# Pacing the sums' transfers by landed weight blocks, and ending the last row tile in two column halves

## The chip, the cores and the metric

The kernel runs on one core of one Trainium2 chip. The metric is the device time of one execution in microseconds (us).

## What is computed

One layer of a hybrid decoder trunk for 512 positions and 1024 channels, all in float32. Only the last part matters for the change:

```python
def conv_ffn(h, w_up, conv_w, w_down):
    up = causal_dwconv(h @ w_up, conv_w)
    gate, val = jnp.split(up, [D_FF], axis=-1)
    return (jax.nn.silu(gate) * val) @ w_down
...
    mix = jax.nn.sigmoid(ga) * y_a + jax.nn.sigmoid(gb) * y_b
    x = x + mix @ w_o[l]
    h = rmsnorm(x, norm_ffn_g[l])
    x = x + conv_ffn(h, w_up[l], ffn_conv_w[l], w_down[l])
    return rmsnorm(x, norm_final_g)
```

Ahead of it stand the projections of the normed input (`w_in`), a gated delta rule, and the products with `w_a_out` and `w_b_out`.

## The kernel before

Each product is made of three matmuls of rounded parts (high by high, high by low, low by high), so every weight block is split on the chip: ScalarE casts it to a high part `wh` (line 140), VectorE subtracts that to get the low part `wl` (line 141). The work is a list of jobs. A job has one weight block of 1 MB, loaded by SyncE's queue (SP) into one of two `raw` buffers, and a `use` that issues its matmuls. `run_jobs` goes through the list: while job i computes, block i+1 is split and block i+2 is loaded. Every 2048 columns of matmul a `tick` takes one step from several queues of small tasks.

Many products save multiplications by Strassen-like forms. Some jobs (`sum_job`) form the sums of weight quarters on VectorE from `raw` (line 161), and put several accumulations into the left half L and the right half R of one PSUM bank A. Between two of them VectorE reads the right half of A (line 283), and the matmuls that follow write the left half:

```python
            def s12():
                act.copy(out=u[:, L], in_=A[:, L])
                dve.tensor_tensor(out=u[:, R], in0=A[:, R], in1=u[:, L], op=ALU.add)
...
            while not done.done:
                advance(evacs, 1)
            times(A[:, L], "12", quarter(1, 0), False)
```

For `w_o` and `w_down` the sums of quarters are formed in DRAM instead, by 112 transfers of 256 KB that GpSimd (POOL) issues (line 1036; `ov`, `ol` for `w_o`, `dv`, `df`, `dl` for `w_down`), most of them adding to what is there. `Sums.form` yields twice after each, and `tick` steps that queue, `adds`, once. On POOL itself nothing ties a transfer to a tick: each waits only for one of eight landing semaphores (DMASW0 to 7) to be free, and for sums that it reads.

The program's order is: delta rule and its projections (to about 300 us), then 24 jobs of `w_in`, `w_a_out` and `w_b_out` (about 310 to 530 us), the product with `w_o` (to 610 us), 22 jobs of `w_up` (to 820 us), and `w_down` in jobs of a 512-column form.

The end is the last `w_down` job, `use_l`: for row tiles 2 and 3 it adds 12 matmuls of 512 columns to the bank of the left half (columns 0 to 511) of that tile; the right half was finished earlier (`fin2_hi`). Then `fin2` runs for each tile: VectorE adds the bank to `x1` (line 1536), ScalarE squares it in place and sums (line 1537), VectorE multiplies by the final gain (1538) and folds the sum into `r` (1541), POOL takes r to the power -1/2 (1543), VectorE scales one half and ScalarE the other (1544, 1545), and SP stores both (1547).

Of the kernel before, what the change touches and what calls it, by code (L numbers as in the profile page):

```python
# [9 lines left out]
F32 = mybir.dt.float32  # L10
# [19 lines left out]
Y_F = (5, 4, 6, 3)  # L30
WARM = 3
WQ = 12
Y_M = 10


# [24 lines left out]
def layer_kernel(ctx, tc, x, norm_mix_g, w_in, w_ab, conv_a_w, gdn_conv_w, gdn_A_log, gdn_dt_bias,  # L60
# [64 lines left out]
    class Block:  # L125
        def __init__(self, src, quarter=(4, P)):
            self.src, self.quarter = src, quarter
            self.raw, self.ready, self.lead = None, False, 2
            self.wh, self.wl = {}, {}

        def load(self):
# [52 lines left out]
    class FormBlock(Block):  # L184
        def __init__(self, runs, names, lead, place):
            super().__init__(None, (S,))
            self.runs, self.names, self.lead, self.place = runs, names, lead, place

        def load(self):
            if self.raw is not None:  # L190
# [13 lines left out]
    def run_jobs(jobs):  # L204
        jobs[1][0].load()
        for i, (block, use) in enumerate(jobs):
            Task(block.split()).finish()
            drain(splits)
            if i + 1 < len(jobs):
                splits.append(Task(jobs[i + 1][0].split()))  # L210
            for j, (later, _) in enumerate(jobs[i + 2:i + 5]):
                if later.lead >= j + 2:
                    later.load()
            use(block.wh, block.wl)


    def piece(w, j, k):
# [797 lines left out]
    class Sums:  # L1015
# [205 lines left out]
        put(xs, slot, 2, 2, 1, xv[:, :, 0, 0])  # L1221
        yield

    def times(o, xs, slot, i, tau, wh, wl, start=False, stop=False, free=False):
        xh, xl = (e[:, slot, i, tau * P:(tau + 1) * P] for e in xs)
        for k, (a, b) in enumerate(((xl, wh), (xh, wl), (xh, wh))):
            mm(o, a, b, start and k == 0, stop and k == 2, free)
# [6 lines left out]
    def times_b(banks, xs, slot, names, tau, wh, wl, q=None, start=False, stop=False):  # L1234
        for name, i in names:
            o, w = banks["11" if name == "21" else name][tau], name if q is None else (name, q)
            times(o, xs, slot, i, tau, wh[w], wl[w], start and name != "21", stop, name == "21")

    def open_banks(banks, names):
        for name in names:  # L1240
# [189 lines left out]
    for g in range(NF // 2):  # L1430
        def up_job(i, c, plain, pre=None):
            if plain:
                return col_job(w_up, i, lambda: st["h2"], c, pre)
            return sum_job(w_up, i, lambda: st["h2"], hsums, c, pair_out)

        last = g == NF // 2 - 1
        gj = up_job(g, gate_c(g), g < 2 or last, (lambda: splits.append(prep_d(prep_a, 0))) if last else None)
        vj = up_job(NF // 2 + g, val_c(g), True)
        jobs += [(gj[0], first_gate), (vj[0], first_val)] if g == 0 else [gj, vj]


# [43 lines left out]
    def use_b(p):  # L1485
        def use(wh, wl):
            if p % 2 == 0 and p // 2 + 1 < N7 // 2:
                splits.append(prep_d(prep_b, p // 2 + 1))
            for name in (*FORMS_T, *FORMS_B):
                for tau in range(2):  # L1490
                    times_b(d_banks, xs(), p % 4, (name,), tau, wh, wl)
            if p == N7 - LAST - 1:
                splits.append(prep_d(prep_b, N7 // 2 - 1))
        return use


    def use_t(q):
# [5 lines left out]
                    fin2(tau, [d_banks["11"][tau], d_banks["22"][tau]])  # L1503
        return use

    def use_l(wh, wl):
        for tau in range(2):
            for i in range(LAST):
                times_b(d_banks, xs(), (N7 - LAST + i) % 4, FORMS_B, tau, wh, wl, i, False, i == LAST - 1)
            fin2(tau + 2, [d_banks["v4"][tau]])  # L1510

    def fin2_hi(t):
        cvp, x1, a = st["cvp"], st["x1"], d_banks["r"][t - 2]
# [10 lines left out]
        yield  # L1524

    def fin2(t, acc):
        cvp, x1 = st["cvp"], st["x1"]
        ss = cvp.tile([P, 2], F32, tag="ss", name=nm("ss"))
        if t < 2:
            o = pair_out()  # L1530
            y, r = [o[:, sl] for sl in HALVES], cvp.tile([P, 1], F32, tag="r", name=nm("r"))
        else:
            y, r = st["y", t], st["r", t]
        for hf, a in enumerate(acc):
            sl = HALVES[hf]
            dve.tensor_tensor(out=x1[:, t, sl], in0=x1[:, t, sl], in1=a, op=ALU.add)  # L1536
            act.activation(out=a, in_=x1[:, t, sl], func=AF.Square, accum_out=ss[:, hf:hf + 1])  # L1537
            dve.tensor_tensor(out=y[hf], in0=x1[:, t, sl], in1=st["gfn"][:, sl], op=ALU.mult)
            if hf < len(acc) - 1:
                dve.tensor_scalar(r, ss[:, hf:hf + 1], 1.0 / D, EPS, op0=ALU.mult, op1=ALU.add)  # L1540
        dve.scalar_tensor_tensor(out=r, in0=ss[:, len(acc) - 1:len(acc)], scalar=1.0 / D, in1=r,  # L1541
                                 op0=ALU.mult, op1=ALU.add)
        pool.tensor_tensor(out=r, in0=r, in1=nhalf[:, 0:1], op=ALU.pow)  # L1543
        dve.tensor_scalar(y[0], y[0], r, None, op0=ALU.mult)
        act.activation(out=y[1], in_=y[1], func=AF.Copy, scale=r)  # L1545
        for sl, e in zip(HALVES, y):
            nc.sync.dma_start(out=out2[t * P:(t + 1) * P, sl], in_=e)


    def down_place(i):  # L1550
# [69 lines left out]
```

## Time and profile before

| | us |
|---|---|
| median of 3 runs (970.35 to 973.03) | 971.42 |
| the profiled execution | 968.61 |
| its span, first to last instruction | 966.9 |
| TensorE (PE) busy | 954.4 |
| VectorE (DVE) busy | 743.9 |
| ScalarE (ACT) busy | 506.3 |
| GpSimd (POOL) busy | 137.1 |

The profiled execution is 1.7 us longer than its span and 2.8 us shorter than the median. A busy PE need not be at its peak, since matmuls overlap; the pace of matmuls is read from their starts.

### The profile page before, as it was taken

The numbers are of one execution on the slowest core, as the hardware profiler recorded it, in microseconds if no ns is written. First come the engines' busy times: TensorE is split into PE (matmuls) and PEld (weight loads), VectorE is DVE, ScalarE is ACT, GpSimd is POOL, SyncE is SP. The second block draws the span as 40 slices with busy tenths as digits, with TensorE's granted clock in tenths as the row PEclk, the third lists the DMA queues.
The fourth block names the chain that finished last, engine by engine and source line by source line (L and its number), as shares of the span: only waits on it lengthen the run. The fifth ranks groups of instructions, "written<-read, shape, count | busy, mean of one in ns | idle before, by whom it ended". The sixth has DMA issues, their size and how long they took to land. (4 is left out here: it accounts for less than half of the span.)

```text
span 966.9 us, 16043 instructions
## 1 busy us (share of the span) xinstructions
PE 954.4 (99%) x6166; PEld 826.9 (86%) x6166; DVE 743.9 (77%) x1397; ACT 506.3 (52%) x1071; POOL 137.1 (14%) x213
## 2 busy tenths in 40 slices
PE   8999999999999999999999999999999999999996
PEld 6888887987878889899988888998889999888885
DVE  6868686896635968799773479999988888969785
ACT  7795556575444434344651235645645455546463
POOL 3330300202002334234320000100000000000000
PEclk9999999999999999999999999999999999999999
DMA  6443312222222989999995235432232323177342
GB/s 226 156 138 115 100 53 88 74 75 75 55 86 76 226 228 252 252 200 260 275 260 150 87 107 220 164 119 88 88 131 87 129 90 132 44 253 235 99 132 87
DMA packets 51628, 138.10 MB, mean 143 GB/s; under 512 B 21691, under 2 KB 22112, under 8 KB 42848
## 3 DMA queue, kind: packets, MB, share of 16 engines
q1 hardware_dynamic: 39008, 107.72, 32.5%
q0 software_dynamic: 12544, 29.37, 14.8%
q8 instruction: 48, 0.79, 0.3%
q14 instruction: 28, 0.23, 0.1%
HBM read 133.64 MB, written 32.78 MB: 172 GB/s over the span
## 5 line engine op out<-in xcount | busy, mean ns | idle before, releaser
L108 PE MATMUL ps<-hT,wh 128*128 128x512 f32 (+1 forms) x1104 | 318.6, 368 | 1.2 <-DVE u L283 0.8
L140 ACT CAST wh<-raw 128x512 fp32r<-128x512 f32 x350 | 203.6, 618 | 214.3 <-PE ps L108 141.0
L141 DVE TENSOR_TENSOR wl<-raw,wh 128x512 fp32r<-128x512 f32 x350 | 232.3, 688 | 62.4 <-ACT wh L140 60.2
L108 PEld LDWEIGHTS ps<-hT,wh 128*128 128x128 f32 x1104 | 196.9, 189 | 30.1 <-DVE u L283 1.0
L108 PE MATMUL ps<-hT,wl 128*128 128x512 f32 (+1 forms) x552 | 195.2, 362 | 0.0
L108 PE MATMUL ps<-h,wh 128*128 128x512 f32 (+1 forms) x704 | 177.9, 341 | 0.3 <-DVE h L1317 0.3
L108 PEld LDWEIGHTS ps<-h,wh 128*128 128x128 f32 x704 | 122.4, 189 | 15.5 <-DVE h L1317 0.5
L108 PEld LDWEIGHTS ps<-hT,wl 128*128 128x128 f32 x552 | 104.4, 189 | 13.8
L108 PE MATMUL ps<-h,wl 128*128 128x512 f32 (+1 forms) x352 | 114.7, 341 | 0.0
L108 PE MATMUL ps<-wh,xs 128*128 128x512 f32 x312 | 96.2, 389 | 0.0
L108 PEld LDWEIGHTS ps<-h,wl 128*128 128x128 f32 x352 | 66.7, 190 | 7.6
L108 PEld LDWEIGHTS ps<-wh,xs 128*128 128x128 f32 x312 | 58.6, 188 | 12.1
L108 PE MATMUL ps<-wl,xs 128*128 128x512 f32 x156 | 60.7, 389 | 0.0
L108 PE MATMUL ps<-ts,wh 128*128 128x256 f32 x320 | 59.2, 283 | 0.0
L328 DVE SCALAR_TENSOR_TENSOR cv<-ps,wA,cv 128x511 f32<-128x511 f32 (+2 forms) x72 | 53.2, 741 | 4.0 <-ACT cv L325 3.8
L140 ACT CAST wh<-raws 128x512 fp32r<-128x512 f32 x66 | 39.2, 619 | 26.2 <-PE ps L108 12.1
L141 DVE TENSOR_TENSOR wl<-raws,wh 128x512 fp32r<-128x512 f32 x66 | 42.8, 685 | 12.1 <-ACT wh L140 12.1
L108 PEld LDWEIGHTS ps<-ts,wh 128*128 128x128 f32 x320 | 50.6, 192 | 0.0
L1543 POOL TENSOR_TENSOR r<-r,nhalf 128x1 f32<-128x1 f32 x4 | 2.2, 540 | 338.2 <-PE ps L108 331.2
L161 DVE TENSOR_TENSOR raw<-raw 128x512 f32<-128x512 f32 x72 | 49.4, 686 | 0.9
L108 PE MATMUL ps<-us,wh 128*128 128x256 f32 x256 | 47.4, 283 | 0.0
L1036 POOL DMA_DIRECT2D dv<-in_w_down_dram x50 | 35.4, 712 | 58.9 <-issue 58.4
(309 smaller groups left out, 1549.8 us busy)
## 6 DMA issues: line engine op xcount, KB each, us to landing
raw<-in_w_in_dram SPq DMA_DIRECT2D x35, 1024.0 KB, 5.5
raw<-in_w_up_dram SPq DMA_DIRECT2D x22, 1024.0 KB, 4.9
dv<-in_w_down_dram POOLq DMA_DIRECT2D x50, 256.0 KB, 7.8
raws<-dv SPq DMA_DIRECT2D x8, 768.0 KB, 7.0
ov<-in_w_o_dram POOLq DMA_DIRECT2D x20, 256.0 KB, 7.1
raws<-in_w_down_dram SPq DMA_DIRECT2D x10, 512.0 KB, 5.1
raw<-in_w_a_out_dram SPq DMA_DIRECT2D x4, 1024.0 KB, 7.7
raw<-in_w_b_out_dram SPq DMA_DIRECT2D x4, 1024.0 KB, 8.5
```

The source lines that it names most:

```text
L108: pe.matmul(o, lhsT=a, rhs=b, start=start, stop=stop, skip_group_check=free)
L140: act.copy(out=wh, in_=src)
L141: dve.tensor_tensor(out=wl, in0=src, in1=wh.bitcast(F32), op=ALU.subtract)
L161: dve.tensor_tensor(out=r[q], in0=a, in1=b, op=op)
L328: dve.scalar_tensor_tensor(out=dst[:, sh:], in0=src[:, :S - sh], scalar=wcol(j), in1=dst[:, sh:], op0=ALU.mult, op1=ALU.add)
L1036: tc.keep_in_program_order(pool.dma_start(out=self.at(g, to), in_=src, **kw))
L1543: pool.tensor_tensor(out=r, in0=r, in1=nhalf[:, 0:1], op=ALU.pow)
```

## The change

Transfers: `adds` is no longer stepped by `tick`. Ahead of the `use` of job i, `feed` makes POOL copy one element of the block of job i+2 (it has to have landed for that) and then issue the next three transfers. It does so where that block is a plain one (`fed`: all of `w_in`, `w_a_out`, `w_b_out`, and `w_up` from its second pair on). There are 38 such copies.

Tail: `use_l` writes its own ending. Tile 3 gets its left half in two halves of 256 columns, 12 matmuls each, and `fin2`'s steps for that tile are made once per half; VectorE, ScalarE, POOL and SP keep the order in which the code is written. The last store goes out on ScalarE's queue. `fin2` is left for tiles 0 and 1 with the same instructions. The `stop` flag set at an earlier job issues nothing.

```diff
@@ tick
         advance(sums_of, 1)
-        advance(adds, 1)
@@ run_jobs
                 if later.lead >= j + 2:
                     later.load()
+            if adds and i + 2 < len(jobs) and jobs[i + 2][0].fed:
+                feed(jobs[i + 2][0].raw)
             use(block.wh, block.wl)
+    def feed(raw):
+        el = raw[0:1, 1].rearrange("p k n -> p (k n)") if len(raw.shape) == 4 else raw[0:1, 1]
+        tc.keep_in_program_order(pool.tensor_copy(out=gate, in_=el[:, 0:1]))
+        advance(adds, FEED)
@@ Sums.form
                         tc.keep_in_program_order(pool.dma_start(out=self.at(g, to), in_=src, **kw))
                         yield
-                        yield
@@ use_l
-        for tau in range(2):
-            for i in range(LAST):
-                times_b(d_banks, xs(), (N7 - LAST + i) % 4, FORMS_B, tau, wh, wl, i, False, i == LAST - 1)
-            fin2(tau + 2, [d_banks["v4"][tau]])
+        def part(t, e, cols, between):
+            a, r = d_banks["v4"][t - 2], st["r", t]
+            ss = st["cvp"].tile([P, 2], F32, tag="ss", name=nm("ss"))
+            for i in range(LAST):
+                times_b(d_banks, xs(), (N7 - LAST + i) % 4, FORMS_B, t - 2, wh, wl, i, False, i == LAST - 1, cols)
+            dve.tensor_tensor(out=x1[:, t, cols], in0=x1[:, t, cols], in1=a[:, cols], op=ALU.add)
+            act.activation(out=a[:, cols], in_=x1[:, t, cols], func=AF.Square, accum_out=ss[:, e:e + 1])
+            between()
+            dve.scalar_tensor_tensor(out=r, in0=ss[:, e:e + 1], scalar=1.0 / D, in1=r, op0=ALU.mult, op1=ALU.add)
+        def between():
+            mult(3, slice(0, HS))
+            scale(2, 1, False, nc.sync)
+            scale(2, 0, True, nc.sync)
+        with tc.manual_schedule(engines={mybir.EngineType.DVE, mybir.EngineType.Activation, mybir.EngineType.Pool,
+                                         mybir.EngineType.SP}):
+            part(2, 0, slice(0, S), lambda: mult(2, slice(0, S)))
+            power(2)
+            part(3, 0, slice(0, HS), between)
+            part(3, 1, slice(HS, S), lambda: None)
+            power(3)
+            mult(3, slice(HS, S))
+            scale(3, 0, False, nc.sync)
+            scale(3, 1, True, nc.scalar)
```

On POOL, around the end of `w_o`'s sums and the start of `w_down`'s, before (a name in brackets behind "waits" is the semaphore waited for):

```order
L1036 DMA ol<-in_w_o_dram 128x512 [waits DMASW0_49]
L1036 DMA ol<-in_w_o_dram 128x512 [waits DMASW1_49]
L1036 DMA ol<-in_w_o_dram 128x512 [waits DMASW2_49]
L1036 DMA ol<-in_w_o_dram 128x512 [waits DMASW3_49]
L1036 DMA dv_371<-in_w_down_dram 128x512 x2
L1036 DMA dv_372<-in_w_down_dram 128x512 x2
L1036 DMA dv_373<-in_w_down_dram 128x512 [waits DMASW4_49]
```

and of the change (DMAHW is the landing of a block on SP's queue):

```order
L223 COPY gate<-raw_5142 1x1 [waits DMAHW4_49,Pool_49]
L1046 DMA ol<-in_w_o_dram 128x512 [waits DMASW2_49]
L1046 DMA ol<-in_w_o_dram 128x512 [waits DMASW3_49]
L1046 DMA dv_372<-in_w_down_dram 128x512
L223 COPY gate<-raw_5286 1x1 [waits DMAHW5_49,Pool_49]
L1046 DMA dv_372<-in_w_down_dram 128x512
L1046 DMA dv_373<-in_w_down_dram 128x512 x2
L223 COPY gate<-raw_5422 1x1 [waits DMAHW6_49,Pool_49]
```

A copy that waits for a weight block now stands ahead of each three transfers; their own order is the same. 21 copies with 63 transfers come ahead of the `w_o` stage's powers on POOL, and 17 copies with the other 49 transfers behind them, among the jobs of `w_up`.

On PE, at the end of the program, the change puts 24 matmuls of 256 columns into the bank `ps_9764` of tile 3, where 12 of 512 columns without any wait stood. These are the end of the first half and the start of the second:

```order
L108 MATMUL ps_9764<-wh_10149,xs_9112 128x256
L108 MATMUL ps_9764<-wl_10150,xs_9111 128x256
L108 MATMUL ps_9764<-wh_10149,xs_9111 128x256
L108 MATMUL ps_9764<-wh_10109,xs_9112 128x256 [waits Activation_49]
L108 MATMUL ps_9764<-wl_10110,xs_9111 128x256
L108 MATMUL ps_9764<-wh_10109,xs_9111 128x256
```

The first matmul of the second half waits for ScalarE; its operands `wh_10109` and `xs_9112` were used 12 matmuls earlier without a wait.

On VectorE, the end of the program before (tile 2 from the third row on, tile 3 from `ps_9725` on):

```order
L1536 TENSOR_TENSOR x_6441<-x_6441,ps_9724 128x512 [waits PE_49]
L1544 TENSOR_SCALAR o_10123<-o_10123,r_10124 128x512 [waits Pool_49]
L1538 TENSOR_TENSOR y_9803<-x_6441,gfn 128x512 [waits DVE_49]
L1541 SCALAR_TENSOR_TENSOR r_9805<-ss_10150,r_9805 128x1 [waits Activation_49]
L1544 TENSOR_SCALAR y_9803<-y_9803,r_9805 128x512 [waits Pool_49]
L1536 TENSOR_TENSOR x_6441<-x_6441,ps_9725 128x512 [waits PE_49]
L1538 TENSOR_TENSOR y_9827<-x_6441,gfn 128x512 [waits DVE_49]
L1541 SCALAR_TENSOR_TENSOR r_9829<-ss_10172,r_9829 128x1 [waits Activation_49]
L1544 TENSOR_SCALAR y_9827<-y_9827,r_9829 128x512 [waits Pool_49]
```

and of the change:

```order
L1544 SCALAR_TENSOR_TENSOR r_9844<-ss_10179,r_9844 128x1 [waits Activation_49]
L1541 TENSOR_TENSOR x_6414<-x_6414,ps_9764 128x256 [waits PE_49]
L1523 TENSOR_TENSOR y_9866<-x_6414,gfn 128x256 [waits DVE_49]
L1530 TENSOR_SCALAR y_9843<-y_9843,r_9844 128x512 [waits Pool_49]
L1544 SCALAR_TENSOR_TENSOR r_9868<-ss_10197,r_9868 128x1 [waits Activation_49]
L1541 TENSOR_TENSOR x_6414<-x_6414,ps_9764 128x256 [waits PE_49]
L1544 SCALAR_TENSOR_TENSOR r_9868<-ss_10218,r_9868 128x1 [waits Activation_49]
L1523 TENSOR_TENSOR y_9866<-x_6414,gfn 128x256 [waits DVE_49]
L1530 TENSOR_SCALAR y_9866<-y_9866,r_9868 128x512 [waits DVE_49,Pool_49]
```

Tile 3's first addition has moved ahead of tile 2's scaling, and there are now two additions and two folds into `r` for tile 3. Before these rows the two programs have the same rows on PE, VectorE, ScalarE and SP.

## Rows read from the trace of the kernel before

**Rows 1.** The page: PE's share, and DMA engines' busy tenths in 40 slices.

```profile
PE 954.4 (99%) x6166; PEld 826.9 (86%) x6166; DVE 743.9 (77%) x1397; ACT 506.3 (52%) x1071; POOL 137.1 (14%) x213
...
DMA  6443312222222989999995235432232323177342
```

**Rows 2.** Windows of 20 us: stretch, length, busy by engine (count), clock, DMA.

```profile
380.00:400.00 20.00, 19.25 (x148) 18.50 (x147) 15.08 (x27) 7.95 (x17) 7.82 (x13) 1.00 0.99 285
420.00:440.00 20.00, 20.00 (x169) 20.00 (x168) 17.96 (x32) 8.27 (x18) 7.60 (x11) 1.00 0.95 202
700.00:720.00 20.00, 20.00 (x129) 18.30 (x128) 17.71 (x30) 10.30 (x20) 0.00 (x0) 1.00 0.30 106
```

**Rows 3.** Timeline of ACT, DVE and PE, 390 to 396 us (start, length).

```profile
390.77 1.14 ACT L140 CAST wh<-raw 128x512 fp32r<-128x512 f32 x2 [4.47 <-DMA raw<-in_w_in_dram]
...
392.75 2.15 DVE L161 TENSOR_TENSOR raw<-raw 128x512 f32<-128x512 f32 x3
...
393.89 0.64 PE L108 MATMUL ps<-hT,wh 128*128 128x256 f32 x4
394.81 0.42 DVE L283 TENSOR_TENSOR u<-ps,u 128x256 f32<-128x256 f32 x1
...
395.28 0.39 PE L108 MATMUL ps<-hT,wh 128*128 128x256 f32 x1 [0.76 <-DVE u L283]
```

**Rows 4.** DMA issues (median us to landing): 340 to 520, 381 to 382, 660 to 820 us; queue of 340 to 520.

```profile
q0 software_dynamic: 10622, 24.79, 66.7%
...
dv<-in_w_down_dram POOLq DMA_DIRECT2D x50, 256.0 KB, 7.8
raw<-in_w_in_dram SPq DMA_DIRECT2D x11, 1024.0 KB, 8.4
...
raw<-in_w_in_dram SPq DMA_DIRECT2D x1, 1024.0 KB, 9.2
...
raw<-in_w_up_dram SPq DMA_DIRECT2D x16, 1024.0 KB, 4.9
```

**Rows 5.** Timeline of the last 9 us (start, length).

```profile
958.93 0.39 PE L108 MATMUL ps<-wh,xs 128*128 128x512 f32 x1
959.10 0.16 DVE L1541 SCALAR_TENSOR_TENSOR r<-ss,r 128x1 f32<-128x1 f32 x1 [0.28 <-ACT ps L1537]
959.91 0.49 DVE L1544 TENSOR_SCALAR y<-y,r 128x512 f32<-128x512 f32 x1 [0.65 <-POOL r L1543]
960.32 0.68 DVE L1536 TENSOR_TENSOR x<-x,ps 128x512 f32<-128x512 f32 x1
...
961.09 0.60 ACT L1537 ACTIVATE ps<-x 128x512 f32<-128x512 f32 x1 [0.46 <-DVE x L1536]
961.63 0.19 ACT L1537 ACTIVATION_READ_ACCUMULATOR ps<-x 128x1 f32 x1
961.85 0.16 DVE L1541 SCALAR_TENSOR_TENSOR r<-ss,r 128x1 f32<-128x1 f32 x1
962.09 0.54 POOL L1543 TENSOR_TENSOR r<-r,nhalf 128x1 f32<-128x1 f32 x1 [2.21 <-DVE r L1541]
962.66 0.72 ACT L1545 ACTIVATE y<-y,r 128x512 f32<-128x512 f32 x1 [0.85 <-POOL r L1543]
...
963.18 0.81 SPq L1547 DMA_DIRECT2D out_dram<-y  x2
```

**Rows 6.** Half-width operations on a bank, 300 to 520 us (ns min/median/max).

```profile
L282 ACT COPY u<-ps x10: 360/372/374, 359.2 to 472.7; 128x256 f32<-128x256 f32 x10
L283 DVE TENSOR_TENSOR u<-ps,u x10: 416/417/425, 359.8 to 473.1; 128x256 f32<-128x256 f32 x10
```

**Rows 7.** Windows at the end, columns as in the second group.

```profile
962.00:963.00 1.00, 0.00 (x0) 0.00 (x0) 0.34 (x2) 0.34 (x1) 0.54 (x1) 0.59 0.67 250
...
964.50:965.00 0.50, 0.00 (x0) 0.00 (x0) 0.00 (x0) 0.00 (x0) 0.00 (x0) 0.50 1.04 389
965.00:965.50 0.50, 0.00 (x0) 0.00 (x0) 0.00 (x0) 0.00 (x0) 0.00 (x0) 0.50 0.81 303
```

More of the change, by code (lines that the diff above doesn't have):

```diff
@@ L32 @@
 WQ = 12
+FEED = 3
 Y_M = 10
@@ L186, in __init__ @@
             super().__init__(None, (S,))
-            self.runs, self.names, self.lead, self.place = runs, names, lead, place
+            self.runs, self.names, self.lead, self.place, self.fed = runs, names, lead, place, False
         def load(self):
@@ L1222, in prep_b, with times @@
         yield
-    def times(o, xs, slot, i, tau, wh, wl, start=False, stop=False, free=False):
+    def times(o, xs, slot, i, tau, wh, wl, start=False, stop=False, free=False, cols=slice(0, S)):
         xh, xl = (e[:, slot, i, tau * P:(tau + 1) * P] for e in xs)
         for k, (a, b) in enumerate(((xl, wh), (xh, wl), (xh, wh))):
-            mm(o, a, b, start and k == 0, stop and k == 2, free)
+            mm(o[:, cols], a, b[:, cols], start and k == 0, stop and k == 2, free)
     def times_a(banks, xs, slot, wh, wl, start, stop):
@@ L1232, in times_a, with times_b @@
                 times(banks[name][tau], xs, slot, i, tau, wh[name], wl[name], start, stop)
-    def times_b(banks, xs, slot, names, tau, wh, wl, q=None, start=False, stop=False):
+    def times_b(banks, xs, slot, names, tau, wh, wl, q=None, start=False, stop=False, cols=None):
         for name, i in names:
             o, w = banks["11" if name == "21" else name][tau], name if q is None else (name, q)
-            times(o, xs, slot, i, tau, wh[w], wl[w], start and name != "21", stop, name == "21")
+            times(o, xs, slot, i, tau, wh[w], wl[w], start and name != "21", stop, name == "21" or bool(cols),
+                  cols or slice(0, S))
     def open_banks(banks, names):
@@ L1438, in layer_kernel @@
         vj = up_job(NF // 2 + g, val_c(g), True)
+        gj[0].fed = vj[0].fed = g > 0
         jobs += [(gj[0], first_gate), (vj[0], first_val)] if g == 0 else [gj, vj]
@@ L1490, in use @@
                 for tau in range(2):
-                    times_b(d_banks, xs(), p % 4, (name,), tau, wh, wl)
+                    times_b(d_banks, xs(), p % 4, (name,), tau, wh, wl, None, False,
+                            p == N7 - LAST - 1 and name in FORMS_B)
             if p == N7 - LAST - 1:
@@ L1506, in use_l, with mult, scale, power @@
     def use_l(wh, wl):
-        for tau in range(2):
-            for i in range(LAST):
-                times_b(d_banks, xs(), (N7 - LAST + i) % 4, FORMS_B, tau, wh, wl, i, False, i == LAST - 1)
-            fin2(tau + 2, [d_banks["v4"][tau]])
+        x1, gfn = st["x1"], st["gfn"]
+        def mult(t, cols):
+            dve.tensor_tensor(out=st["y", t][0][:, cols], in0=x1[:, t, cols], in1=gfn[:, cols], op=ALU.mult)
+        def scale(t, hf, on_act, queue):
+            y, r = st["y", t][hf], st["r", t]
+            if on_act:
+                act.activation(out=y, in_=y, func=AF.Copy, scale=r)
+            else:
+                dve.tensor_scalar(y, y, r, None, op0=ALU.mult)
+            queue.dma_start(out=out2[t * P:(t + 1) * P, HALVES[hf]], in_=y)
+        def power(t):
+            pool.tensor_tensor(out=st["r", t], in0=st["r", t], in1=nhalf[:, 0:1], op=ALU.pow)
+        def part(t, e, cols, between):
+            a, r = d_banks["v4"][t - 2], st["r", t]
+            ss = st["cvp"].tile([P, 2], F32, tag="ss", name=nm("ss"))
+            for i in range(LAST):
+                times_b(d_banks, xs(), (N7 - LAST + i) % 4, FORMS_B, t - 2, wh, wl, i, False, i == LAST - 1, cols)
[17 more added lines that the diff above has]
+            scale(3, 1, True, nc.scalar)
     def fin2_hi(t):
@@ L1526, in fin2 @@
     def fin2(t, acc):
-        cvp, x1 = st["cvp"], st["x1"]
+        cvp, x1, y = st["cvp"], st["x1"], pair_out()
         ss = cvp.tile([P, 2], F32, tag="ss", name=nm("ss"))
[L1529 to L1542, printed above, removed]
+        r = cvp.tile([P, 1], F32, tag="r", name=nm("r"))
+        for hf, sl in enumerate(HALVES):
+            dve.tensor_tensor(out=x1[:, t, sl], in0=x1[:, t, sl], in1=acc[hf], op=ALU.add)
+            act.activation(out=acc[hf], in_=x1[:, t, sl], func=AF.Square, accum_out=ss[:, hf:hf + 1])
+            dve.tensor_tensor(out=y[:, sl], in0=x1[:, t, sl], in1=st["gfn"][:, sl], op=ALU.mult)
+            if hf == 0:
+                dve.tensor_scalar(r, ss[:, 0:1], 1.0 / D, EPS, op0=ALU.mult, op1=ALU.add)
+        dve.scalar_tensor_tensor(out=r, in0=ss[:, 1:2], scalar=1.0 / D, in1=r, op0=ALU.mult, op1=ALU.add)
         pool.tensor_tensor(out=r, in0=r, in1=nhalf[:, 0:1], op=ALU.pow)
[L1544 to L1547, printed above, removed]
+        dve.tensor_scalar(y[:, HALVES[0]], y[:, HALVES[0]], r, None, op0=ALU.mult)
+        act.activation(out=y[:, HALVES[1]], in_=y[:, HALVES[1]], func=AF.Copy, scale=r)
+        for sl in HALVES:
+            nc.sync.dma_start(out=out2[t * P:(t + 1) * P, sl], in_=y[:, sl])
     def down_place(i):
```

3 lines of the change are left out of this document (2 added, 1 removed).

## The prediction, made before the changed kernel was run

> **What bounds the kernel now.** I read the page first. TensorE is busy for 954.4 of 966.9 us, so only what PE loses between its first and last matmul, and what lies outside them, can be won [rows 1]. The DMA line of the same page is near full in slices 14 to 21 (of 24.2 us each), some 190 us in which the 112 transfers of the sums are under way beside the weight blocks. The second view is the windows. At 420 to 440 us, inside that stretch, PE has no idle time and starts 169 matmuls of 256 columns, one per 0.118 us; that is its pace when nothing holds it. At 380 to 400 us it is idle for 0.75 us with the DMA engines at 0.99. At 700 to 720 us, among the jobs of `w_up`, the DMA share is 0.30 and PE is full [rows 2]. So the crowded stretch costs PE one short stall.
>
> The third view, the timeline, shows that stall. ScalarE waits 4.47 us for a block of `w_in` and starts its split at 390.77. VectorE then has the block's sums to make until 394.9, and its read of bank A (L283) comes only at 394.81, behind them. The four matmuls from 393.89 start 0.12 apart, so the next was due at 394.37; it starts at 395.28 and lasts 0.39 instead of 0.28 [rows 3]. Price: 0.91 + 0.11 = 1.0 us. That block took 9.2 us from issue to landing; 11 blocks of `w_in` in the stretch took 8.4 in the median, 16 of `w_up` later 4.9 [rows 4]. The block is late because it shares the DMA engines with the sums.
>
> The fourth view is the end. The last matmul starts at 958.93 and ends at 959.32. Tile 3's addition starts at 960.32 only, since VectorE had tile 2's scaling (959.91, after the wait for POOL) ahead of it. Then come the square (961.09, its sum read out by 961.82), the fold (961.85), the power (962.09), ScalarE's scaling (962.66 to 963.38) and the stores, issued from 963.18 [rows 5]. The DMA engines are full at 964.5 to 965 and carry the two halves of 256 KB until about 965.4 [rows 7], and the span ends at 966.9.
>
> **The change, part by part.** *Pacing.* POOL used to issue whenever a landing semaphore came free. Now three transfers follow each landed block. In the 180 us from 340 on their queue moved 24.79 MB, 94.6 transfers of 0.262 MB, in 66.7% of the engines' time [rows 4]: 120 / 94.6 = 1.27 us of all sixteen for one. Three cost 3.8 us per job; a job is 84 matmuls of 256 columns (9.9 us) or 48 of 512 (10.9 us). Before, one started every 180 / 94.6 = 1.9 us, so five or six fell into the time of a job. With a block's 4.9 us ahead of them, 4.9 + 3.8 = 8.7 us fit into a job, so a block should land in about 5 us instead of 8.4, and ScalarE's wait of 4.47 us should go. What PE gets back is the 1.0 us stall and no more, because in the rest of the stretch it lost nothing. Bounds: 0 if a straggling transfer still meets that block, 1.0 if not; I take 1.0, as the block's lateness of 9.2 - 4.9 = 4.3 us is nearly all of the 4.47 us wait.
>
> The 49 transfers that move among the jobs of `w_up` raise its DMA share by 3.8 / 10.4 = 0.37 to about 0.67. They end by job 67, four jobs before the first block of `w_down` sums is loaded, so no sum is late. The 38 copies are new. The nearest row for a tiny POOL operation is the power's 0.54 us [rows 5]; 38 of them are 20 us on an engine that is busy for 137 [rows 1]. Behind a copy stand only transfers, and the four powers of the `w_o` stage, whose last copy ahead waits for a block that the `w_b_out` jobs had to have before that stage began. Cost between 0 and 0.54 each on POOL alone; on the path nothing, since the transfers that they delay are needed later by several jobs.
>
> *The tail.* Moving tile 3's addition ahead of tile 2's scaling takes out VectorE's wait. But the order of PE shows a new wait: the first matmul of the second half waits for ScalarE. Its operands were used before, so what it waits for is the bank: ScalarE writes the squares of the first half into it. The row of the stall at 395.28 shows the same: a matmul into the left half of bank A was held by L283, which reads the right half [rows 3]. So the wait goes by the whole bank, and the second half can't start while the first is being read and squared.
>
> I walk the new chain. Nothing ahead of tile 2's fold at 959.10 changes. The first half of tile 3 starts at 958.93 - 11 x 0.227 = 956.44 and ends at 956.44 + 11 x 0.12 + 0.28 = 958.04, long before VectorE is free. Its addition starts right behind the fold, at 959.17, and takes 0.42 (the half-width addition from a bank [rows 6]): 959.59. ScalarE starts the square at 959.63; a half-width operation takes 0.36 to 0.37 [rows 6], the read-out starts 0.06 before its end and takes 0.19 [rows 5]: 960.12. PE starts again at 960.17, its second matmul 0.22 later, the twelfth at 961.59, ending at 961.87. From there as before: addition 961.90 to 962.32, square and read-out to 962.84, fold at 962.87, power 0.24 later at 963.11, scaling 0.57 after that at 963.68. Before it was 962.66. So the path grows by 1.02 us, where the reorder alone would have saved.
>
> *The last store on ScalarE's queue.* Both halves' stores are issued 0.4 us apart at most, and the transfers fill the engines from the first on (512 KB until 965.4 [rows 7]). So the end follows the first store, which moves by 1.02. An issue from ScalarE is not in this trace; the nearest row is SP's 0.81 for two [rows 5]. Overlapping them saves 0 to 0.4; I take 0, since the engines are full. The rewritten `fin2` and the flag issue nothing else.
>
> *The rule on banks.* The Trainium skill, page "PSUM — Partial Sum Buffer", section "PSUM bank collisions raise a hardware error", says to guard PSUM by bank and quadrant, "not by address", since two engines on one bank collide even at different columns. That speaks against an ending in halves of one bank, and the trace's wait at 395.28 (0.76 us) agrees with it. By that rule the tail is the chain above; by addresses it would be the second rival below.
>
> **The sum.** -1.0 (stall) + 1.0 (tail) + 0 (copies, store) = 0.0 us against the profiled execution's 968.61. That execution lies 2.8 us below the median of 971.42, and the sum is carried over to the median: 971.4.
>
> **The rivals.**
> 1. *More was lost to late blocks than the profile shows.* The timed runs are up to 2.8 us longer than the profiled one. If that is stalls like the one at 395.28, pacing takes it too: 971.4 - 2.8 = 968.6. For it: the crowded stretch is the place that varies. Against: in this profile 11 late blocks made one stall.
> 2. *The halves don't wait for one another.* Then PE ends at 959.5, VectorE does the second addition behind tile 2's scaling and the fold (960.39 to 960.81), the square ends at 961.34, the fold stands at 961.37 and the scaling at 962.18, 0.48 earlier than before: -1.0 - 0.5, 969.9. Against it stands the row on PE in the order.
> 3. *The clock drops in the new gap.* The granted clock averages 0.59 between 962 and 963 [rows 7], so it fell to 1.2 GHz some 2.9 us after the last matmul had ended. The gap here is 960.17 - 958.04 = 2.1 us, shorter than that. If it fell all the same, the twelve matmuls would take 0.24 instead of 0.12 each (an estimate: half the clock, twice the time): +1.4, 972.8.
> 4. *Slower: the sums crowd the jobs of `w_up`.* Transfers that straggle past a job's end meet the next block, as at 390.77, where 4.3 us of lateness cost 1.0 us. Eight jobs there form sums; if each were hit, 8 us are lost and the time is 979.4. It decides from 3 stalls on. For it: VectorE has little air there (17.7 of 20 us [rows 2]). Against: the copy holds the transfers back until the block in flight has landed, and 8.7 us fit into a job.
>
> **How the numbers follow.** Forecast 0.60, rivals in their order 0.12, 0.10, 0.09, 0.09. About 0.3% (2.9 us) is what a measurement can tell from no change, so faster means below 968.5 and slower above 974.3. Rival 1 lies on the border: 0.07 of it counts as faster, and 0.02 for the rest. Slower takes most of rival 4: 0.08. The other 0.83 is no change. The range must hold rivals 2 and 3 and the scatter of a median (about 1 us), and stops at rival 1's edge: 968.8 to 973.4. The forecast's own is 970.4 to 972.4.
>
> **What would show it.** Right: the DMA line of slices 14 to 21 falls from 9 to about 7 and that of slices 27 to 34 rises from 2 or 3 to about 6; blocks of `w_in` land in about 5 us; no PE wait on L283; in the tail a PE gap of some 2.1 us ahead of the second half, and the last scaling 4.6 us after tile 2's fold (963.68 - 959.10) instead of 3.6. Wrong: no gap on PE in the tail, blocks of `w_up` that land after 7 us or more with ScalarE waiting for them, or PE idle in the `w_up` jobs.

## The result, and the profile of the changed kernel

The change made the kernel slower: 973.56 us in the median of 11 runs (972.86 to 975.32) against 971.3 of 11 runs of the kernel before (968.88 to 973.03). The ratio over all of these runs is 1.0032, with a 95% interval of 1.0022 to 1.0042; the quotient of the two medians is 1.0023, and the ratios of the experiments below are likewise not quotients of medians. The median lies just above the forecast range of 968.8 to 973.4, and the interval reaches to either side of the 0.3% that the prediction took as the border between no change and slower. The profiled execution took 972.86 us, its span is 971.2 against 966.9.

First the page, to be read against [rows 1]: the line of PE, the DMA line in 40 slices (24.3 us each), and the group of the new copies (count | busy, mean ns | idle before them and its releaser).

```profile
PE 957.7 (99%) x6178; PEld 825.8 (85%) x6178; DVE 744.4 (77%) x1400; ACT 507.3 (52%) x1073; POOL 153.2 (16%) x251
...
DMA  6443312222221447766786445584765674085232
...
L223 POOL COPY gate<-raw 1x1 f32<-1x1 f32 x38 | 16.5, 435 | 277.8 <-DMA raw<-in_w_in_dram 121.3
```

PE is busy 3.3 us longer. The DMA line did what was forecast: slices 14 to 21 fell from 8 or 9 to between 4 and 8, slices 27 to 34 rose from 2 or 3 to between 4 and 8. POOL's 277.8 us of waiting for blocks is on an engine with time to spare.

The windows answer to [rows 2], with two late stretches added. First the changed kernel (stretch, length, busy by engine with counts, clock, DMA share, GB/s):

```profile
380.00:400.00 20.00, 20.00 (x155) 19.32 (x155) 17.11 (x30) 9.38 (x18) 4.58 (x8) 1.00 0.80 209
...
500.00:520.00 20.00, 20.00 (x87) 16.10 (x86) 6.78 (x11) 3.42 (x6) 5.90 (x10) 1.00 0.82 201
...
700.00:720.00 20.00, 20.00 (x130) 18.27 (x129) 17.11 (x29) 10.09 (x19) 5.43 (x8) 1.00 0.80 180
900.00:920.00 20.00, 20.00 (x87) 16.05 (x87) 16.43 (x25) 9.21 (x17) 0.00 (x0) 1.00 0.25 87
```

Then two of these stretches in the kernel before:

```profile
500.00:520.00 20.00, 20.00 (x90) 16.55 (x89) 7.57 (x12) 4.38 (x8) 3.66 (x5) 1.00 0.95 232
...
900.00:920.00 20.00, 20.00 (x90) 16.57 (x89) 17.46 (x27) 10.43 (x19) 0.00 (x0) 1.00 0.25 79
```

At 380 to 400 us PE's 0.75 us of idle time are gone. But at 500 to 520 and at 900 to 920 us the windows hold 87 matmuls of 512 columns where they held 90 (the count takes in those under way at the window's start, so the pace is better read from starts). PE is busy all the time, its clock is at 1.00, and at 900 us the DMA share is 0.25 in both: nothing waits, and yet the next matmul comes later. At 500 us the change still alters the transfers (DMA share 0.82 instead of 0.95), but at 900 us none of the changed steps is under way. The timeline shows it on single rows; first before, then after:

```profile
900.22 0.39 PE L108 MATMUL ps<-wl,xs 128*128 128x512 f32 x1
...
901.58 0.39 PE L108 MATMUL ps<-wl,xs 128*128 128x512 f32 x1
```

```profile
900.05 0.39 PE L108 MATMUL ps<-wl,xs 128*128 128x512 f32 x1
...
901.45 0.39 PE L108 MATMUL ps<-wl,xs 128*128 128x512 f32 x1
```

Every third matmul uses `wl`, so between these rows lie six starts: 1.36 / 6 = 0.227 us before, 1.40 / 6 = 0.233 after. The length of a row (0.39) shows nothing; the pace is in the starts.

The tail answers to [rows 5], in order of time:

```profile
960.60 0.28 PE L108 MATMUL ps<-wh,xs 128*128 128x256 f32 x1
...
962.06 0.16 DVE L1544 SCALAR_TENSOR_TENSOR r<-ss,r 128x1 f32<-128x1 f32 x1 [0.28 <-ACT ps L1542]
962.13 0.42 DVE L1541 TENSOR_TENSOR x<-x,ps 128x256 f32<-128x256 f32 x1
...
962.64 0.39 ACT L1542 ACTIVATE ps<-x 128x256 f32<-128x256 f32 x1 [0.62 <-DVE x L1541]
...
963.21 0.38 PE L108 MATMUL ps<-wh,xs 128*128 128x256 f32 x1 [2.33 <-ACT ps L1542]
...
964.60 0.27 PE L108 MATMUL ps<-wh,xs 128*128 128x256 f32 x1
964.91 0.42 DVE L1541 TENSOR_TENSOR x<-x,ps 128x256 f32<-128x256 f32 x1 [1.44 <-PE ps L108]
...
966.21 0.66 POOL L1534 TENSOR_TENSOR r<-r,nhalf 128x1 f32<-128x1 f32 x1 [3.37 <-DVE r L1544]
966.90 0.72 ACT L1528 ACTIVATE y<-y,r 128x512 f32<-128x512 f32 x1 [0.96 <-POOL r L1534]
```

The second half waits 2.33 us for ScalarE's square of the first, and the last scaling comes 966.90 - 962.06 = 4.84 us after tile 2's fold, where it was 3.56.

To see where the 4.3 us of the span arise, the same matmuls' starts in two profiled executions are subtracted. In us against the kernel before, at PE's matmul number (and its time before); "after" is the changed kernel, and experiments of the next section stand beside it:

```
matmul               100     800    2200    3600    4600    6100
time before         20.3   115.6   274.8   475.2   669.9   944.2
after               0.51    0.47    0.55   -1.36    0.50    2.52
e1_no_new_tile      2.14    3.12    3.14    2.12    2.12    2.12
e2_pad32            0.35    0.33    0.41   -0.06    1.79    3.81
e4_pacing_only      1.88    1.88    1.91    0.92    0.92    0.92
e7_pacing_and_r.    0.62    1.65    1.71    0.69    0.70    0.70
e10_sums_192       -0.03    1.06    1.10   -3.06   -3.35   -5.65
```

What is lost or gained in the first 75 us differs between executions: e1 and e7 have the same code there, and lose 3.12 and 1.65 us by matmul 800. Behind that, the changed kernel wins 1.91 us by matmul 3600, then loses 1.86 and 2.02 in two stretches in which PE's waits sum to at most 0.2 us.

### The profile page after: what moved, and what is told of

Same layout as the page of the kernel before. It is cut to its first block, busy times and chain, and to the rows that moved or that the text cites. A ratio compares the mean times of both kernels' runs of the same rounds, so it can differ in the third digit from the quotient of the medians.

```text
span 971.2 us, 16170 instructions
## 1 busy us (share of the span) xinstructions
PE 957.7 (99%) x6178; PEld 825.8 (85%) x6178; DVE 744.4 (77%) x1400; ACT 507.3 (52%) x1073; POOL 153.2 (16%) x251
## 4 chain that ended last, share of the span: by engine, by line
PE 91%; DVE 3%; ACT 1%; issue 1%; POOL 1%; POOLq 0%
PE ps L108 83%; PE ps L681 1%; PE ps L716 1%; DVE wl L141 1%; PE ps L890 1%; PE ps L910 1%; DVE h L1327 0%; PE ps L899 0%; DVE hn L1313 0%; PE ps L878 0%; PE ps L877 0%; PE ps L854 0%; PE ps L848 0%; POOL r L1311 0%; PE ps L792 0%
## 5 line engine op out<-in xcount | busy, mean ns | idle before, releaser
L108 PE MATMUL ps<-wh,xs 128*128 128x512 f32 (+1 forms) x320 | 98.7, 390 | 2.3 <-ACT ps L1542 2.3
L108 PE MATMUL ps<-wl,xs 128*128 128x512 f32 (+1 forms) x160 | 62.3, 389 | 0.0
L223 POOL COPY gate<-raw 1x1 f32<-1x1 f32 x38 | 16.5, 435 | 277.8 <-DMA raw<-in_w_in_dram 121.3
L108 PE MATMUL ps<-yas,wh 128*128 128x512 f32 x128 | 40.4, 395 | 0.0
```

Of the source, the lines that this page charges most:

```text
L223: tc.keep_in_program_order(pool.tensor_copy(out=gate, in_=el[:, 0:1]))
```

## The experiments

The first theory behind them: the copies' target `gate` does the harm. It is a 4-byte tile, allocated ahead of everything else in the constants, and takes 32 bytes of each partition. In the built program every tile that is allocated from the left (constants, `raw`, `wh`, `wl`, `hT`) has moved up by 32 bytes: `wh` from 19168 to 19200. The tiles of the pools on the right (`ts`, `us`, `yas`, `mix`, `xs`) stay where they were. The products that slowed down take one operand from each side. The rivals: the copies themselves, the new traffic in the DMA engines, or the tail.

**e1_no_new_tile.** The changed kernel, with the copies into an element that exists already.

```diff
-    gate = const.tile([1, 1], F32, name="gate")
...
-        tc.keep_in_program_order(pool.tensor_copy(out=gate, in_=el[:, 0:1]))
+        tc.keep_in_program_order(pool.tensor_copy(out=phalf[0:1, 0:1], in_=el[:, 0:1]))
```

> The change with one edit: POOL's copy writes into an element of a constant that is no longer read, so the new 4-byte tile is gone and every tile has the address that it has in the kernel before. Theory A (the new tile moved the tiles allocated from the left by 32 bytes, and 512-column matmuls that read one operand from a moved tile and the other from an unmoved one take 0.2333 us instead of 0.2267): some 620 such matmuls lose 4.1 us, so the pace is 0.2267 again at 500 to 530 and from 855 us on, and the time is about 3.5 to 4 us below the change: 969.5 to 970, a ratio to the kernel before of 0.998 to 0.9995. Theory B (the transfers or POOL's copies slow PE): the pace stays at 0.2333 and the time at 973.5, a ratio of 1.002 to 1.003.

Measured: 971.83 us, ratio 1.0005 (0.9994 to 1.0017). The 38 copies, the transfers and the tail are all there, and the pace is back at 0.227 us, with 90 matmuls in each of the two windows:

```profile
500.00:520.00 20.00, 20.00 (x90) 16.57 (x89) 6.99 (x13) 4.57 (x8) 5.45 (x8) 1.00 0.80 201
900.00:920.00 20.00, 20.00 (x90) 16.57 (x89) 16.30 (x26) 9.42 (x17) 0.00 (x0) 1.00 0.30 97
```

The pace is what theory A expected; the time is above its 969.5 to 970. The profiled span of 970.6 holds 3.1 us lost in the first 75 us; from there to matmul 6100 it gains 1.0 on the kernel before, where the changed kernel loses 2.05. So the tile, and not the copies, costs the 3 us of the profile.

**e2_pad32.** The kernel before, with an unused tile ahead of the constants.

```diff
+    pad = const.tile([P, 1], F32, name="pad")
```

> The kernel before with one unused 4-byte tile per partition added to the constants, nothing else: all engines' instructions stay the same, the tiles allocated from the left move by 32 bytes. Theory A: the 512-column pace is 0.2333 us at 500 to 530 and from 855 us on, time 3 to 4 us above the kernel before, a ratio of 1.003 to 1.004. Theory B: no difference, a ratio of 1.000 within 0.001.

Measured: 972.56 us, ratio 1.0016 (1.0004 to 1.0029). The windows of this kernel:

```profile
500.00:520.00 20.00, 20.00 (x88) 16.09 (x87) 7.56 (x12) 4.56 (x8) 4.90 (x6) 1.00 0.94 217
...
900.00:920.00 20.00, 20.00 (x87) 16.05 (x86) 15.80 (x23) 8.53 (x14) 0.00 (x0) 1.00 0.30 94
```

An unused tile alone brings the slow pace, 88 and 87 matmuls instead of 90, and in the table above +1.85 and +2.02 us in the same two stretches as in the changed kernel. The timed medians differ by 1.7 us, less than the 3 to 4 expected and than the profiles show (3.2, below); the interval reaches to 2.8.

**e4_pacing_only.** The kernel before, with the transfers paced as in e1; against e1 only the end is undone.

```diff
-            part(2, 0, slice(0, S), lambda: mult(2, slice(0, S)))
...
-            scale(3, 1, True, nc.scalar)
+        for tau in range(2):
+            for i in range(LAST):
+                times_b(d_banks, xs(), (N7 - LAST + i) % 4, FORMS_B, tau, wh, wl, i, False, i == LAST - 1)
+            fin2(tau + 2, [d_banks["v4"][tau]])
```

> The kernel before with the pacing of the sums' transfers alone (the copy writes into a constant that is no longer read, so no address changes; the end is that of before). Theory A with the sum of the prediction: the stall at 395 us goes, 1.0 us less, a ratio of 0.999. Theory B: PE's later matmuls are slower, 3 us more, a ratio of 1.003. Third theory: the timed runs lost more to late blocks than the profile, up to 3 us less, a ratio of 0.997.

Measured: 969.67 us (968.26 to 969.94), ratio 0.9988 (0.9977 to 0.9999). No PE wait on VectorE's read of the bank is left; in the table the kernel gains 0.99 us between matmuls 2200 and 3600 and is level from matmul 100 to 2200 and from 3600 to 6100. Behind that it loses 0.25: tile 0's power, the first on POOL in the tail, begins 0.59 us after tile 0's fold instead of 0.37. It is 0.59 or 0.60 in all six kernels with pacing, and 0.37 or 0.38 in the six without; why stays open.

**e5_tail_only.** The kernel before, with the new end alone; against the changed kernel:

```diff
+        advance(adds, 1)
...
-            if adds and i + 2 < len(jobs) and jobs[i + 2][0].fed:
-                feed(jobs[i + 2][0].raw)
...
-    gate = const.tile([1, 1], F32, name="gate")
...
+                        yield
```

> The kernel before with the new end alone (two halves of columns, orders by hand, last store from ScalarE's queue), no pacing, no new tile. Theory of the bank wait: PE waits 2.3 us between the halves for ScalarE's square, the last scaling comes 4.84 us after tile 2's fold instead of 3.56, and the time grows by 1.3 us, a ratio of 1.0013. If the halves did not wait for one another it would fall by 0.5, a ratio of 0.9995.

Measured: 972.1 us, ratio 1.0027 (1.0011 to 1.0042), so slower as expected for halves that wait; the profiled execution, of 977.23 us, is the longest of its 12. Its tail (fold of tile 2, start of the second half, last scaling), and the windows of that half:

```profile
965.92 0.16 DVE L1543 SCALAR_TENSOR_TENSOR r<-ss,r 128x1 f32<-128x1 f32 x1 [0.28 <-ACT ps L1541]
...
967.07 0.39 PE L109 MATMUL ps<-wh,xs 128*128 128x256 f32 x1 [2.23 <-ACT ps L1541]
...
971.17 0.72 ACT L1527 ACTIVATE y<-y,r 128x512 f32<-128x512 f32 x1 [0.96 <-POOL r L1533]
```

```profile
967.00:968.00 1.00, 0.94 (x7) 0.94 (x8) 0.33 (x2) 0.62 (x2) 0.00 (x0) 1.00 0.52 193
968.00:969.00 1.00, 1.00 (x7) 0.85 (x5) 0.00 (x0) 0.00 (x0) 0.00 (x0) 0.58 0.90 332
```

The scaling comes 5.25 us after the fold, 0.4 more than in the changed kernel: here the granted clock fell to 1.2 GHz (0.58, then 0.50) about 1.1 us after PE had started again, and the last matmuls lie 0.22 instead of 0.12 apart. In e1, PE had waited 2.46 us and the clock stayed at 1.00:

```profile
962.62 0.39 PE L108 MATMUL ps<-wh,xs 128*128 128x256 f32 x1 [2.46 <-ACT ps L1541]
...
964.00:965.00 1.00, 0.31 (x3) 0.11 (x1) 0.42 (x1) 0.14 (x1) 0.00 (x0) 1.00 1.02 383
```

So the price of the gap differs between executions. In e5 PE also waited 3.4 us for VectorE near 395 us, and the clock then fell to 1.2 GHz for some 3 us:

```profile
PE ps L109 <- DVE u L291: 3.4, 1, 3.4
```

```profile
402.00:405.00 3.00, 3.00 (x10) 2.41 (x10) 3.00 (x7) 0.93 (x2) 1.72 (x3) 0.51 0.86 122
```

**e6_reorder_only.** The kernel before, with the hand order, but tile 3's left half in one piece of 512 columns: one addition, one square, one fold. Against e5:

```diff
-            mult(3, slice(0, HS))
...
-            part(3, 0, slice(0, HS), between)
-            part(3, 1, slice(HS, S), lambda: None)
+            part(3, 0, slice(0, S), between)
...
-            mult(3, slice(HS, S))
+            mult(3, slice(0, S))
```

> The kernel before with the hand order of the new end and its store from ScalarE's queue, but tile 3's left half in one piece of 512 columns: no wait of PE for ScalarE, tile 3's addition ahead of tile 2's scaling. The last scaling comes 2.6 us after tile 2's fold instead of 3.56 (tile 3's addition at 959.35 instead of 960.32), so 1.0 us less, a ratio of 0.999. If the end were set by something else than VectorE's order, no change.

Measured: 970.47 us, ratio 0.9995 (0.9978 to 1.0012), which by itself tells nothing. The profile does (fold of tile 2, last multiplication by the gain, last power, last scaling):

```profile
960.43 0.16 DVE L1543 SCALAR_TENSOR_TENSOR r<-ss,r 128x1 f32<-128x1 f32 x1 [0.28 <-ACT ps L1541]
...
962.29 0.68 DVE L1522 TENSOR_TENSOR y<-x,gfn 128x512 f32<-128x512 f32 x1
962.45 0.93 POOL L1533 TENSOR_TENSOR r<-r,nhalf 128x1 f32<-128x1 f32 x1 [1.25 <-DVE r L1543]
...
963.41 0.72 ACT L1527 ACTIVATE y<-y,r 128x512 f32<-128x512 f32 x1 [0.62 <-POOL r L1533]
```

2.98 us instead of 3.56: the order alone saves 0.58, and the halves cost 4.84 - 2.98 = 1.86. The expected 2.6 was missed by POOL's power, which takes 0.93 us here where it took 0.54 [rows 5]: the hand order puts VectorE's multiplication by the gain behind the last fold, and the power runs beside it. In the kernel before, that multiplication came ahead of the fold.

**e7_pacing_and_reorder.** e1 with e6's end, against the changed kernel:

```diff
-    gate = const.tile([1, 1], F32, name="gate")
...
-        tc.keep_in_program_order(pool.tensor_copy(out=gate, in_=el[:, 0:1]))
+        tc.keep_in_program_order(pool.tensor_copy(out=phalf[0:1, 0:1], in_=el[:, 0:1]))
...
-            mult(3, slice(0, HS))
...
-            part(3, 0, slice(0, HS), between)
-            part(3, 1, slice(HS, S), lambda: None)
+            part(3, 0, slice(0, S), between)
...
-            mult(3, slice(HS, S))
+            mult(3, slice(0, S))
```

> Pacing without a new tile and the hand order without column halves: -1.2 us (the pacing alone as measured) and -1.0 (the order alone), a ratio of 0.9977; no stall at 395 us, 512-column pace 0.2267 everywhere. If the two gains overlap, 0.9988.

Measured: 968.94 us (967.09 to 969.87), ratio 0.9972 (0.996 to 0.9984): faster than the kernel before with the change's own two ideas, without its tile and its halves. The last scaling comes 2.80 us after tile 2's fold, so by this profile the order saves 0.76 and the halves cost 2.04.

**e8_both_sides_32.** The kernel before, both sides moved by 32 bytes. It asks whether the place within 64 bytes sets the pace, which was the theory's form by then.

```diff
+    pad = const.tile([P, 1], F32, name="pad")
...
+        sc.tile([P, 1], F32, name="padr")
...
+        up.tile([P, 1], F32, name="padu")
```

> The kernel before with an unused 4-byte tile in the constants and one in each of the two pools that are allocated from the right, so that the tiles on both sides move by 32 bytes (left up, right down) and all begin at a multiple of 64. If what costs is that a matmul's two operands begin at different places within 64 bytes, the pace is 0.2267 us everywhere and the ratio 1.000 within 0.001. If what costs is that the left tiles moved to a multiple of 64, the pace of yas, mix and xs is 0.2333 as with the pad on one side, and the ratio 1.002 to 1.004.

Measured: 968.13 us, ratio 0.997 (0.9954 to 0.9987). Neither expectation held: `yas` was as slow as with one side moved (233.3 ns), `xs` and `mix` went to 228.9, and the 256-column products to 113.7 ns from 120.0. The tiles on the right are allocated downwards, so the two sides had moved apart, by 64 bytes in all.

**e9_sums_apart.** e7 with `ts` and `us` set 32 bytes into tiles that are 64 bytes longer; `yas`, `mix` and `xs` get the longer tiles too and start at their beginning. `us` is edited as `ts` is here:

```diff
-        st["ts"] = [sc.tile([P, 4, 4, HS], F32R, tag=f"t{i}", name=f"ts{i}") for i in range(2)]
+        st["ts"] = [sc.tile([P, 4112], F32R, tag=f"t{i}", name=f"ts{i}")[:, 8:8+4096].rearrange("p (a b n) -> p a b n", a=4, b=4) for i in range(2)]
```

> The kernel before this one with one more edit: the operands of the 256-column matmuls that hold sums (ts, us) begin 32 bytes into their tiles, so that they begin at another place within 64 bytes than the weights, while yas, mix and xs begin at the same place as the weights. In the change these 256-column matmuls got 1.44 us faster in all when the weights moved by 32 bytes. If that is the same effect of places within 64 bytes, with the opposite sign for 256 columns, the time falls by 1.4 us against the kernel before this one, a ratio to the kernel before of 0.9962 instead of 0.9977; if not, the two agree.

Measured: 972.62 us, ratio 1.0013 (1.0 to 1.0025); 118.7 ns for 256 columns, and 233.2 for 512. The expectation missed. The first tile's extra 64 bytes put the second of each pair elsewhere, and the products take them in turn. With e8 the theory of a place within 64 bytes falls. The mean paces so far could instead be ordered by one quantity: the distance between the address of one matmul's moving operand (the one of 256 or 512 columns) and that of the next one's stationary operand (the one of 128x128 that PEld loads ahead of a matmul), modulo 256 bytes. The next load runs beside a matmul, as these rows of the changed kernel show, which is why the next one's operand was taken:

```profile
963.21 0.38 PE L108 MATMUL ps<-wh,xs 128*128 128x256 f32 x1 [2.33 <-ACT ps L1542]
963.31 0.19 PEld L108 LDWEIGHTS ps<-wl,xs 128*128 128x128 f32 x1
```

That choice is argued, not shown: in all kernels but e9 a matmul's own stationary operand lies at the same distance as the next one's.

**e3_pad64.** The kernel before, with a pad of 64 bytes on the left: another address than in e8, the same distance.

```diff
+    pad = const.tile([P, 16], F32, name="pad")
```

> The kernel before with one unused tile of 64 bytes per partition in the constants: the left tiles move by 64 bytes and begin at 32 beyond a multiple of 64 as before; the right ones stay. If only the distance between a matmul's moving operand and the next stationary one counts, within 256 bytes, this is the case of the pads on both sides: ts and us at 113.5 ns per 256-column matmul instead of 120.0, yas at 233.4 ns instead of 226.7, xs near 226; 2.9 us less in all, a ratio of 0.997. If the place within 64 bytes decides (the first form of the theory), everything is as before, a ratio of 1.000.

Measured: 968.32 us, ratio 0.9985 (0.9975 to 0.9994). All paces are those of e8 to 0.1 ns, though the left tiles stand elsewhere within 64 bytes. The expectation held for `ts`, `us` and `yas`; it missed for `xs` (228.9 instead of near 226), and 0.997 lies outside the interval. Its windows show both signs: 256 columns faster (174 in the window, where the kernel before has 169, as in [rows 2]), 512 columns of `yas` slower (87).

```profile
440.00:460.00 20.00, 20.00 (x174) 20.00 (x173) 19.46 (x34) 8.02 (x16) 7.18 (x12) 1.00 0.97 284
500.00:520.00 20.00, 20.00 (x87) 16.02 (x86) 8.20 (x14) 5.61 (x10) 4.90 (x6) 1.00 0.96 204
```

**e10_sums_192.** e7 with `ts` and `us` 192 bytes into their tiles; the tiles are 256 bytes longer, so that both of a pair keep their distance, and the others stay at distance 0. `us` is edited as `ts` is here:

```diff
-        st["ts"] = [sc.tile([P, 4, 4, HS], F32R, tag=f"t{i}", name=f"ts{i}") for i in range(2)]
+        st["ts"] = [sc.tile([P, 4160], F32R, tag=f"t{i}", name=f"ts{i}")[:, 48:48+4096].rearrange("p (a b n) -> p a b n", a=4, b=4) for i in range(2)]
```

> Pacing without a new tile, the hand order without column halves, and ts and us set 192 bytes into their tiles (which are 256 bytes longer), so that their distance to the weights is 192 bytes within 256; yas, mix and xs stay at distance 0. By distance: 864 matmuls of 256 columns take 113.5 ns instead of 120.0, 5.6 us less than the kernel with pacing and order alone, a ratio to the kernel before of 0.9915. If the distance is not what counts, 0.9972 as that kernel.

Measured: 961.94 us (961.87 to 962.53, 5 runs), ratio 0.9922 (0.991 to 0.9933). It beats both kernels, and the pace came out as expected from the distance alone. Both kinds of product now run at their better pace, 113.7 and 226.7 ns:

```profile
440.00:460.00 20.00, 20.00 (x175) 20.00 (x174) 19.15 (x34) 9.60 (x20) 4.30 (x8) 1.00 0.62 150
500.00:520.00 20.00, 20.00 (x90) 16.57 (x89) 6.75 (x11) 4.57 (x8) 6.40 (x10) 1.00 0.77 184
```

## Why the prediction was wrong, step by step

**The step that failed** is the one on the copies: "on the path nothing". It priced the copies as POOL's work, and there it was right (435 ns each, inside the bounds of 0 and 0.54 us; e1 keeps them and loses nothing between matmuls 800 and 6100). What it didn't look at is what the copy writes: a new tile, and by it the addresses of half the program's tiles. The paces, from the starts of consecutive matmuls in the traces:

```
ns per matmul                       before, e1    after, e2    e3, e8    e10
512 columns, yas                       226.7        233.3       233.3   226.7
512 columns, mix and xs                226.7        233.3       228.9   226.7
256 columns, ts and us                 120.0        118.4       113.7   113.7
```

Products of 512 columns with both operands on the left (`hT`, `h`, `yb`) are at 226.7 to 228 in all of these. 192 matmuls on `yas`, 168 on `mix` and 456 on `xs` lose 6.5 to 6.7 ns each, 5.4 us; 864 on `ts` and `us` gain 1.6 each, 1.4 us: net +4.0. The table of starts gives less. e4 has the pacing without the tile, so what after loses against it is the tile's: (-1.91 + 0.99) + 1.86 + 2.02 = +2.96 to matmul 6100. From there to tile 2's fold the changed kernel loses 0.44 more; e2, with the tile alone, loses 0.21 there, and e4, with the pacing alone, 0.25. So the tile costs +3.2 in the profile.

A smaller misreading: the prediction took 0.118 us as the pace of 256 columns from the 169 matmuls in a window [rows 2]; the starts give 0.120, and a job of 84 takes 10.1 us instead of 9.9. Nothing in the sum hangs on it.

**The stall, -1.0.** Right in place and size: the block of `w_in` that had ScalarE wait 4.47 us [rows 3] now costs 0.2 us, no PE wait on VectorE's read of bank A is left, and e4 gains 0.99 there. The blocks of the stretch land in 4.8 us, forecast about 5, before 8.4 [rows 4]. The changed kernel's rows, ScalarE's waits at 380 to 400 us and the DMA issues at 340 to 520 us:

```profile
ACT wh L140 <- DMA raw<-in_w_in_dram: 0.2, 1, 0.2
```

```profile
raw<-in_w_in_dram SPq DMA_DIRECT2D x11, 1024.0 KB, 4.8
```

**The tail, +1.0.** The mechanism was right, the size a little off: +1.28 (4.84 - 3.56; forecast 4.58 - 3.56 = 1.02). The half-width squares start 0.09 and 0.10 us behind the additions, not 0.04, and the power took 0.66 instead of 0.54, as it now runs beside a multiplication of 256 columns on VectorE (966.05 to 966.47 and 966.21 to 966.87), which the chain left out. The Trainium skill, page "PSUM — Partial Sum Buffer", section "PSUM bank collisions raise a hardware error", says to guard PSUM by bank and not by address; the wait of 2.33 us between two halves with different columns agrees. It is a wait in the program's semaphores, so it shows that the kernel was built by that rule, not what the chip would do without it. The last store on ScalarE's queue gained nothing, as forecast: from the start of the last scaling to the end of the span it takes 971.2 - 966.9 = 4.3 us, and took 966.9 - 962.66 = 4.2 before.

**The sum of the profiled executions**: +0.5 in the first 20 us, -1.0 (stall), +0.25 (the later first power), +3.2 (tile), +1.3 (tail) = +4.25, measured +4.3. In the timed runs e2 (1.0016), e4 (0.9988) and e5 (1.0027) add up to 1.0031; measured 1.0032. With intervals of 0.0011 to 0.0016 to either side of each, so close an agreement is in part luck: e5's 0.0027 is twice what the tail costs in the changed kernel's profile. How the timed cost of the tile (1.7 us by e2, 2.6 by the ratios of after and e1) goes with 3.2 in the profiles is open.

**The rivals.** *More lost to late blocks than the profile shows*: partly right. The stall near 395 us is 0.8 us in the profile of before, 1.0 to 3.6 in five other kernels without pacing (e2, e3, e5, e6, e8), and there is none in the six with it. After the two longest, 3.6 us in e3 and 3.4 in e5, the granted clock also fell to 1.2 GHz for a few matmuls. Pacing takes 1.2 us from the median (e4), not 2.8. But it narrows the scatter: from the lowest to the highest run the six kernels with pacing differ by 0.7 to 3.2 us (e4: 968.26 to 969.94), the five experiments without it by 4.1 to 6.9, and the kernel before, in the four sets of runs of 11 to 35, by 3.7 to 7.9. So the crowded stretch did vary from run to run, as the rival said; that its stalls make the long runs fits this, but the timed runs have no trace that would show it. *The halves don't wait*: no. *The clock drops in the gap*: not in the changed kernel's profile (1.00 until the last matmul), yet in e5's, whose chain is 0.4 us longer rather than the +1.4 worked out, as only its last few matmuls met it. *The sums crowd the jobs of `w_up`*: no. The DMA share rose to 0.80 at 700 to 720 us, not to 0.67, and the blocks of `w_up` land in 5.8 us at 660 to 820 us (before 4.9 [rows 4]), but PE is full there, and e1 and e4 are level from matmul 3600 on. The time came out above the range by a mechanism that was none of the rivals; that the forecast of no change missed by so little is luck, since the tile's cost was not in it at all.

## What to carry to other kernels

A new tile, however small, moves others: when a change allocates something, compare the addresses in the built program, or give a dummy write an element that exists. Where PE is full and yet slower, count matmul starts in equal windows of untouched stretches before looking at waits. Try the distance of the operands' addresses on purpose (from e7 to e10 it was worth more than pacing and order together: 0.9972 to 0.9922), and don't split a bank's columns to overlap engines that wait by bank. Judge a change that takes out irregular waits by the spread of the runs too, and not by the median alone.

## What the runs showed of the hardware

The pace of these float32r matmuls depends on where their two operands lie relative to each other: on the distance of the moving operand's address from the stationary operand's. e3 and e8 have the same distances at different addresses and the same paces; e10 has the distance of `ts` and `us` 192 bytes up where e3 and e8 have it 64 bytes down, with the same 113.7 ns, so it counts modulo 256 bytes as far as that one pair shows. Means over `yas`, `xs`, `ts` and `us`, ns from start to start:

```
distance      0      32     64     192    224
512 cols   226.7  233.3  228.9   233.3  233.3
256 cols   120.0    -      -     113.7  118.4
```

The order is not the same for both widths: 0 is the best distance for 512 columns, and the worst seen for 256. The distances 32 and 64 occurred only where a weight block is the moving operand (`xs`, `mix`), 192 and 224 only where it is the stationary one. e9, whose pairs of tiles lie at two distances (64 and 128, 128 and 192, 160 and 224), runs at 233.2 and 118.7 on average, but single intervals there don't follow the distance: at 128 throughout they alternate between 229 and 238 ns, and `yas` at 192 comes to 229.3 beside its neighbours at 128. So whether it is the matmul's own stationary operand or the next one's, and what in the memory or in PE makes the distances differ, stays open. Clock and DMA share were the same in windows of either pace (1.00, and 0.25 at 900 to 920 us).

POOL's power on a column of 128 numbers took 0.92 us beside VectorE's multiplication of 512 columns by the gain (e6, e7, e9, e10), 0.66 beside one of 256 columns (after, e1, e5), and 0.54 to 0.55 where that multiplication came ahead of the fold (before, e2, e3, e4, e8). ScalarE's scaling, which waits for it, moved with it.

The second surprise is the start: from the first to the hundredth matmul, twelve profiled executions of nearly the same code differ by up to 2.5 us, and three of them (e1, e7, e10) lose about 1.0 us more between 35 and 75 us. The profile of before lies at the low end of these, and 2.8 us below its median; how much of that comes from the start is not shown, since the timed runs have no trace. A single profile can be 2 us off by its start alone.
